# A hybrid decoder layer on one core: where the normalized rows are scaled, stored and cut

## The chip, the cores and the metric

The kernel runs on one core of one Trainium2 chip. A core has a matrix engine (PE, or TensorE), a vector engine (DVE), an activation engine (ACT), a general engine (POOL, or GpSimd), a queue engine that only starts transfers here (SP), and DMA engines that move data between device memory and the on-chip memory. Each engine works through its own queue in order; semaphores tie the queues together. The metric is the device time of one execution in microseconds (us); less is better.

## The reference

One decoder layer on 512 tokens of width 1024, all in float32. The input is normalized, and the normalized rows feed a token mixer with two branches and later serve as its residual:

```
h = layer_norm(x, ln_in_g, ln_in_b)
mix = token_mixer(h, ...)          # SSD branch and sliding-window attention branch, gated, projected
h = layer_norm(ALPHA * h + mix, ln_mix_g, ln_mix_b)
ffn = swiglu_ffn(h, ...)
h = layer_norm(ALPHA * h + ffn, ln_ffn_g, ln_ffn_b)
```

The attention has 16 heads of 64 columns over blocks of 128 queries, each block seeing its own block and the one before it, under a causal mask and a window mask.

## The kernel before

Tokens are cut in four tiles of 128 rows (`x_t[0]` to `x_t[3]`, 1024 columns each, in the tile `x_sb`). Weights stream in units of 128x1024: SP loads a unit into `w_raw`, ACT rounds it to `w_hi` (line 135), DVE forms the rest `w_lo` (line 136), and PE multiplies with three matmuls of 128x512 for each block of 128 (lines 149 to 151). PE's instruction order is the order of the program text. So is that of ACT and DVE in the first stage (lines 553 to 632). Elsewhere a scheduler orders the queues of ACT, DVE and POOL by priority and by when it expects an instruction to be ready, so an instruction far down in the text can come up early.

**First stage.** Four loads bring `x`. DVE takes mean and variance of tiles 0, 2 and 3 (`ln_stats`), ACT those of tile 1 (`act_stats`). Tiles 0 and 1 are normalized on ACT by `row_scale` (line 563), tiles 2 and 3 on DVE by `normalize` (line 201). `row_scale(1)` is called between the two halves of tile 3's statistics, so its ACT instruction stands ahead of the square root that tile 3 needs (line 197). Then `units.prepare(1)` splits the first weight unit `kv_w`, and `hT_tile(k)` transposes column block k of all four tiles on PE (line 217), rounds it on ACT (line 222) and forms the rest on DVE (lines 226 and 227). Dummy transposes (`warm_up`, line 548) fill PE before and between the first matmuls. Behind this stage POOL stores the four normalized tiles to device memory (`x_d`, line 635).

**Attention.** The loop over t has eight steps of two heads each. The scores are scaled on POOL (line 467), transposed on PE (line 480), copied to `pT` by ACT (line 482), masked by POOL (`affine_select`, line 483) and DVE (line 486), and multiplied with the values by PE (`ps_o`, line 493). Between these PE runs other products out of a list (`fill`, `need`): the q, x and gate products.

**Row scaling.** Behind the loop in the text POOL reads each stored tile back into `row` (line 703), multiplies it by the gain (line 704), adds the bias (line 705) and stores it to `h_d` (line 706), which is read again only for the residual of the mixer, far later. `row` has two buffers, which it shares with the scores `sc`; the gain and bias rows share buffers with `q_f`. After attention PE runs the products `yb` on `attT`, and then the SSD stage.

Of the kernel before, what the change touches and what calls it, by code (L numbers as in the profile page):

```python
# [14 lines left out]
AF = mybir.ActivationFunctionType  # L15
# [3 lines left out]
P = 128  # L19
S = 512  # L20
D = 1024
# [41 lines left out]
def kernel(  # L63
# [13 lines left out]
    nc = tc.nc  # L77
# [6 lines left out]
    def gap(pl, size):  # L84
# [13 lines left out]
        out=tri, in_=tri, pattern=[[1, P]], compare_op=ALU.is_ge, fill=0.0,  # L98
# [87 lines left out]
    def ln_stats(pl, src, between=None, cuts=(0, 512, 1024)):  # L186

        n = len(cuts) - 1
        st = pl.tile([P, 4, 6], F32, name="ln_st", tag="ln_st", bufs=2)[:, 0:n]
        for i in range(n):  # L190
            nc.vector.bn_stats(out=st[:, i], in_=src[:, cuts[i]:cuts[i + 1]])
            if i == 0 and between:
                between()
        mv = pl.tile([P, 2], F32, name="ln_mv", tag="ln_mv", bufs=3)
        nc.vector.bn_aggr(out=mv, in_=st)
        rs = pl.tile([P, 1], F32, name="ln_rs", tag="ln_rs", bufs=3)
        nc.scalar.activation(rs, mv[:, 1:2], AF.Sqrt, bias=eps_t, scale=1.0)
        return mv[:, 0:1], rs

    def normalize(src, mean, rs):  # L200
        nc.vector.tensor_scalar(
            out=src, in0=src, scalar1=mean, scalar2=rs, op0=ALU.subtract, op1=ALU.mult)
# [26 lines left out]
    def split_to(hi, lo, src):  # L229
        nc.scalar.copy(out=hi, in_=src)  # L230
        nc.vector.tensor_sub(out=lo, in0=src, in1=hi.bitcast(F32))

    x_d = dram.tile([S, D], F32, name="x_d")
# [35 lines left out]
    def axt(shape, name):  # L269
        return psX.tile(shape, F32, name=name, tag="ax")  # L270
# [111 lines left out]
    x_sb = at.tile([P, NT, D], F32, name="x_sb", tag="attT_lo")  # L382
# [86 lines left out]
        att_p[t] = sc  # L469
        yield  # L470

    att_p, last_exp = {}, [None]

    def weighted_values(t):
        kv, sc = t // 4, att_p.pop(t)
        pT = at.tile([P, 2, 7, P], F32, name="pT", tag="pT", bufs=1)
        for j in range(2):
            ps = axt([P, NT, P], "ps_pt")
            for n in range(NT):
                nc.tensor.transpose(ps[:, n], sc[:, j, n], ident)  # L480

            nc.scalar.copy(out=pT[:, j, 1::2], in_=ps[:, 1:])
            nc.gpsimd.affine_select(
                out=pT[:, j, 1::2], in_=pT[:, j, 1::2], pattern=[[0, NT - 1], [-1, P]], compare_op=ALU.is_ge,
                fill=0.0, base=-1, channel_multiplier=1)
            nc.vector.tensor_tensor(
                out=pT[:, j, 0::2], in0=ps, in1=tri.unsqueeze(1).broadcast_to([P, NT, P]), op=ALU.mult)
            yield
        ps = axt([P, S], "ps_o")
        for n in (0, 2, 1, 3):  # L490
            w = min(2, NT - n)
            for j in range(2):
                nc.tensor.matmul(  # L493
                    ps[64 * j:64 * j + 64, n * P:(n + w) * P], v_sb[:, n, kv * 64:kv * 64 + 64],
                    pT[:, j, 2 * n:2 * n + w].rearrange("p b k -> p (b k)"),
                    start=(n == 0), stop=(n == NT - 1))
        split_to(attT_hi[:, t], attT_lo[:, t], ps)
        yield
# [44 lines left out]
    x_t = [x_sb[:, ti] for ti in range(NT)]  # L543

    def warm_up(n):

        for _ in range(n):
            nc.tensor.transpose(ps_warm, ident, ident)

    def hT_tile(k, **kw):  # L550
        return transposed_k(psX, f_t[:, k % 3], x_t, k, 0, hT_hi[:, k], hT_lo[:, k], nc.vector, **kw)

    with tc.manual_schedule(engines={mybir.EngineType.DVE, mybir.EngineType.Activation}):

        nc.scalar.activation(at.tile([P, 1], F32, name="root"), eps_t, AF.Sqrt)
        warm_up(40)
        nmr = at.tile([P, NT + 1], F32, name="nmr")

        def row_scale(ti, mean, rs):
            nc.vector.reciprocal(rs, rs)  # L560
            nc.vector.scalar_tensor_tensor(
                out=nmr[:, ti:ti + 1], in0=mean, scalar=-1.0, in1=rs, op0=ALU.mult, op1=ALU.mult)
            nc.scalar.activation(x_t[ti], x_t[ti], AF.Identity, bias=nmr[:, ti:ti + 1], scale=rs)

        def act_stats(src):

            junk = f_t.rearrange("p a b -> p (a b)")[:, 0:D]
            mv = at.tile([P, 2], F32, name="ln_mv", tag="ln_mv", bufs=3)
            nc.scalar.activation(junk, src, AF.Identity, scale=1.0 / D, accum_out=mv[:, 0:1])
            nm = nmr[:, NT:NT + 1]  # L570
            nc.scalar.mul(out=nm, in_=mv[:, 0:1], mul=-1.0)
            nc.scalar.activation(junk, src, AF.Square, bias=nm, accum_out=mv[:, 1:2])
            rs = at.tile([P, 1], F32, name="ln_rs", tag="ln_rs", bufs=3)
            nc.scalar.activation(rs, mv[:, 1:2], AF.Sqrt, bias=eps_t, scale=1.0 / D)
            return mv[:, 0:1], rs

        row_scale(0, *ln_stats(at, x_t[0]))
        st1 = act_stats(x_t[1])
        st2 = ln_stats(at, x_t[2])
        st3 = ln_stats(at, x_t[3], partial(row_scale, 1, *st1))  # L580
        nc.vector.reciprocal(st2[1], st2[1])
        normalize(x_t[2], *st2)
        nc.vector.reciprocal(st3[1], st3[1])
        for a in (slice(0, 256), slice(256, D)):
            normalize(x_t[3][:, a], *st3)
        units.prepare(1)
        hT_tile(0, between=lambda i: warm_up(36 * (i == 0)))
        nc.scalar.copy(out=wdt_hi, in_=wdt_sb)
        nc.vector.tensor_sub(out=wdt_lo, in0=wdt_sb, in1=wdt_hi.bitcast(F32))
        units.prepare(2)  # L590
        hT_tile(1)
        units.prepare(3)
        w += [units.next(u, ahead=0) for u in (U_K, U_V, U_Q)]

        def part(k, o, a, b):

            nc.tensor.matmul(ps[o], w[o - 1][a][:, k], (hT_hi, hT_lo)[b][:, k],
                             start=k + a + b == 0, stop=k == KD - 1 and b == 1)

        def part_dt(k, b):  # L600

            nc.tensor.matmul(ps[0], wdt_r[:, k], (hT_hi, hT_lo)[b][:, k],
                             start=k + b == 0, stop=k == KD - 1 and b == 1)


        for o, a, b in ((1, 0, 0), (1, 1, 0), (2, 0, 0), (1, 0, 1), (2, 0, 1)):
            part(0, o, a, b)
            warm_up(3 * (b == 0))
        part_dt(0, 0)
        part_dt(0, 1)  # L610
        part(0, 2, 1, 0)
        for k in range(KD):
            if k > 0:

                for o in (1, 2):
                    for a in range(2):
                        part(k, o, a, 0)
                part_dt(k, 0)
                if k == 1:
                    part(0, 3, 0, 0)  # L620
                    part(0, 3, 0, 1)
                part(k, 3, 0, 0)
                part_dt(k, 1)
                for o in (1, 2):
                    part(k, o, 0, 1)
                if k == 1:
                    part(0, 3, 1, 0)
                part(k, 3, 1, 0)
                part(k, 3, 0, 1)
            if k + 2 < KD:  # L630
                dve_ins = hT_tile(k + 2)
            if k in (3, 5):
                units.prepare(4 + k // 5)
    for ti in range(NT):
        nc.gpsimd.dma_start(out=x_d[ti * P:(ti + 1) * P], in_=x_sb[:, ti])
    al_b = at.tile([P, NH], F32, name="al_b")
    snk = at.tile([P, 16], F32, name="snk")
    nsnk = at.tile([P, 16], F32, name="nsnk")
# [58 lines left out]
    gb1 = [at.tile([P, D], F32, name="gb1", tag="q_f", bufs=2) for _ in range(2)]  # L697
    for i, t in enumerate(gb1):
        nc.gpsimd.dma_start(out=t, in_=ln_in[i:i + 1].broadcast_to([P, D]))
    for ti in range(NT):  # L700
        row = at.tile([P, D], F32, name="row", tag="sc", bufs=2)
        rows = slice(ti * P, (ti + 1) * P)
        nc.gpsimd.dma_start(out=row, in_=x_d[rows])
        nc.gpsimd.tensor_mul(row, row, gb1[0])
        nc.gpsimd.tensor_add(row, row, gb1[1])
        nc.gpsimd.dma_start(out=h_d[rows], in_=row)

# [333 lines left out]
    for half in range(2):  # L1041
# [23 lines left out]
        for ti in toks:  # L1065
            hr = res[ti]
            for o in range(2):
                os = slice(o * 512, (o + 1) * 512)
                nc.vector.scalar_tensor_tensor(
                    out=hr[:, os], in0=hr[:, os], scalar=ALPHA, in1=acc[ti][o], op0=ALU.mult, op1=ALU.add)  # L1070
            mean, rs = ln_stats(r3, hr)
# [199 lines left out]
```

## Time and profile before

| what | value |
|---|---|
| median of 3 runs | 1038.83 us (1037.22 to 1038.92) |
| the profiled execution, its own time | 1038.49 us |
| its span, first to last instruction | 1036.6 us |
| mean granted TensorE clock | 0.995 |
| PE busy | 1017.7 us, 98% |
| DVE busy | 596.7 us, 58% |
| ACT busy | 506.1 us, 49% |
| POOL busy | 202.6 us, 20% |

The span is what the profile covers; the execution's own time is 1.9 us more. The busy times say which engine could be the bound; what a stage is worth is read from the waits inside that stage. A granted clock of 1.00 is TensorE at 2.4 GHz, 0.50 at 1.2 GHz.

### The profile page before, as it was taken

How to read it: one execution, taken by the hardware profiler on the slowest of the kernel's cores; microseconds unless marked ns; L12 is line 12 of the kernel's file. 1: busy time of each engine (PE TensorE's matmuls, PEld its weight loads, DVE VectorE, ACT ScalarE, POOL GpSimd, SP SyncE). 2: the span in 40 equal slices, each digit the busy share in tenths (PEclk: the TensorE clock that was granted, in tenths of full speed). 3: DMA queues.
4: the chain of work that ended last, by engine and by line, in shares of the span. 5: the costliest groups of instructions: out<-in, count | busy, mean ns of one | idle time of the engine just before them, and what ended most of it. 6: DMA issues, size and time to landing. Idle time of an engine off the chain costs nothing.

```text
span 1036.6 us, 13203 instructions
## 1 busy us (share of the span) xinstructions
PE 1017.7 (98%) x5044; PEld 839.0 (81%) x5044; DVE 596.7 (58%) x835; ACT 506.1 (49%) x864; POOL 202.6 (20%) x195
## 2 busy tenths in 40 slices
PE   8999999799999999999999999999999999999997
PEld 7888888588887878888888888898888888888885
DVE  6789875143666674685673676646433333332765
ACT  5464567624865785684652633334433332322450
POOL 2011224602215123102313730291000000000000
PEclk9999999899999999999999999999999999999999
DMA  8211224435343432334322254316433333331471
GB/s 314 82 62 62 87 83 135 149 123 158 103 131 96 144 127 98 104 116 139 119 93 82 82 183 162 122 41 208 157 121 105 120 107 117 121 122 61 153 252 43
DMA packets 38799, 126.56 MB, mean 122 GB/s; under 512 B 4528, under 2 KB 5040, under 8 KB 38480
## 3 DMA queue, kind: packets, MB, share of 16 engines
q1 hardware_dynamic: 36080, 116.14, 34.3%
q0 software_dynamic: 2080, 7.47, 2.1%
q10 hardware_dynamic: 576, 2.10, 0.5%
q8 instruction: 40, 0.66, 0.3%
q14 instruction: 23, 0.19, 0.1%
HBM read 119.27 MB, written 6.42 MB: 121 GB/s over the span
## 4 chain that ended last, share of the span: by engine, by line
PE 87%; DMA 3%; DVE 3%; ACT 2%; issue 1%; POOL 1%; SPq 0%; POOLq 0%; ACTq 0%; DVEq 0%
PE ps_mm L149 14%; PE ps_mm L150 13%; PE ps_mm L151 13%; PE ps_ff L149 8%; PE ps_ff L150 8%; PE ps_ff L151 8%; PE ps_da L149 2%; PE ps_da L151 2%; PE ps_da L150 2%; PE ps_mix L149 1%; PE ps_mix L151 1%; PE ps_mix L150 1%; PE ps_yd L836 1%; PE ps_o L493 1%; PE ps_db L150 1%
## 5 line engine op out<-in xcount | busy, mean ns | idle before, releaser
L135 ACT CAST w_hi<-w_raw 128x1024 fp32r<-128x1024 f32 x185 | 193.5, 1050 | 307.5 <-PE ps_ff L150 122.3
L136 DVE TENSOR_TENSOR w_lo<-w_raw,w_hi 128x1024 fp32r<-128x1024 f32 x185 | 234.7, 1273 | 159.0 <-ACT w_hi L135 155.0
L149 PE MATMUL ps_mm<-hT_hi,w_hi 128*128 128x512 f32 x504 | 203.8, 404 | 0.5 <-DVE cacc L371 0.5
L150 PE MATMUL ps_mm<-hT_lo,w_hi 128*128 128x512 f32 x504 | 197.1, 391 | 0.0
L151 PE MATMUL ps_mm<-hT_hi,w_lo 128*128 128x512 f32 x504 | 196.8, 390 | 0.0
L149 PE MATMUL ps_ff<-h2T_hi,w_hi 128*128 128x512 f32 (+1 forms) x384 | 143.2, 373 | 0.0
L150 PE MATMUL ps_ff<-h2T_lo,w_hi 128*128 128x512 f32 (+1 forms) x384 | 142.6, 371 | 0.0
L151 PE MATMUL ps_ff<-h2T_hi,w_lo 128*128 128x512 f32 (+1 forms) x384 | 142.6, 371 | 0.0
L149 PEld LDWEIGHTS ps_mm<-hT_hi,w_hi 128*128 128x128 f32 x504 | 95.0, 188 | 22.8 <-issue 5.1
L151 PEld LDWEIGHTS ps_mm<-hT_hi,w_lo 128*128 128x128 f32 x504 | 94.8, 188 | 20.4
L150 PEld LDWEIGHTS ps_mm<-hT_lo,w_hi 128*128 128x128 f32 x504 | 95.1, 189 | 18.2 <-issue 1.0
L151 PEld LDWEIGHTS ps_ff<-h2T_hi,w_lo 128*128 128x128 f32 x384 | 72.3, 188 | 12.6
L149 PEld LDWEIGHTS ps_ff<-h2T_hi,w_hi 128*128 128x128 f32 x384 | 72.3, 188 | 12.5
L150 PEld LDWEIGHTS ps_ff<-h2T_lo,w_hi 128*128 128x128 f32 x384 | 72.3, 188 | 12.4
L1119 DVE TENSOR_TENSOR sgf<-sgf,ps_ff 128x512 f32<-128x512 f32 x22 | 15.1, 687 | 68.0 <-PE ps_ff L151 68.0
L149 PE MATMUL ps_mm<-yh,w_hi 128*128 128x512 f32 x124 | 49.2, 397 | 0.0
L150 PE MATMUL ps_mm<-yl,w_hi 128*128 128x512 f32 x124 | 48.3, 390 | 0.0
L151 PE MATMUL ps_mm<-yh,w_lo 128*128 128x512 f32 x124 | 48.3, 389 | 0.0
L371 DVE SCALAR_TENSOR_TENSOR cacc<-ps_mm,pc,cacc 128x511 f32<-128x511 f32 (+2 forms) x54 | 39.9, 741 | 9.9 <-ACT cacc L368 9.3
L761 ACT ACTIVATE L<-L,nac 128x128 f32<-128x128 f32 x128 | 40.8, 390 | 5.9 <-POOL L L756 5.6
L780 DVE TENSOR_TENSOR L<-L,cb 128x1024 f32<-128x1024 f32 x16 | 21.7, 1354 | 37.2 <-ACT cb L778 22.0
L756 POOL TENSOR_SCALAR_AFFINE_SELECT L<-L 128x1024 f32<-128x1024 f32 x16 | 18.8, 1176 | 94.0 <-DMA L<-a_d 91.4
(269 smaller groups left out, 1724.3 us busy)
## 6 DMA issues: line engine op xcount, KB each, us to landing
w_raw<-in_wall_dram SPq DMA_DIRECT2D x187, 512.0 KB, 3.5
L<-a_d SPq DMA_DIRECT2D x16, 512.0 KB, 5.4
E<-e_d SPq DMA_DIRECT2D x24, 128.0 KB, 3.5
x_d<-x_sb POOLq DMA_DIRECT2D x4, 512.0 KB, 7.6
row<-x_d POOLq DMA_DIRECT2D x4, 512.0 KB, 4.1
h_d<-row POOLq DMA_DIRECT2D x4, 512.0 KB, 3.3
h_r<-h_d ACTq DMA_DIRECT2D x4, 512.0 KB, 4.2
out_dram<-y_o SPq DMA_DIRECT2D x7, 256.0 KB, 4.0
```

What stands on the lines that cost most here:

```text
L135: (copy or nc.scalar.copy)(out=hi, in_=w)
L136: self.last = (eng or nc.vector).tensor_sub(out=lo, in0=w, in1=hi.bitcast(F32))
L149: nc.tensor.matmul(ps, lh, rh, start=start, stop=False)
L150: nc.tensor.matmul(ps, lh, rl, start=False, stop=False)
L151: nc.tensor.matmul(ps, ll, rh, start=False, stop=stop)
L371: nc.vector.scalar_tensor_tensor(out=acc[:, d:], in0=ps[:, :S - d], scalar=pc[:, cw + 3 - d:cw + 4 - d], in1=acc[:, d:], op0=ALU.mult, op1 ...
L493: nc.tensor.matmul(ps[64 * j:64 * j + 64, n * P:(n + w) * P], v_sb[:, n, kv * 64:kv * 64 + 64], pT[:, j, 2 * n:2 * n + w].rearrange("p b k ...
L756: nc.gpsimd.affine_select(out=Lf, in_=Lf, pattern=[[0, 8], [1, P]], compare_op=ALU.is_ge, fill=-BIG, base=0, channel_multiplier=-1)
L761: nc.scalar.activation(L[:, j, t], L[:, j, t], AF.Exp, bias=nac5[:, g, j, c, t:t + 1], scale=1.0)
L780: nc.vector.tensor_tensor(out=Lf, in0=Lf, in1=cb.unsqueeze(1).broadcast_to([P, 8, P]), op=ALU.mult)
L836: nc.tensor.matmul(psd[64 * j:64 * j + 64, t], X[:, t, j], L[:, j, t], start=True, stop=True)
L1119: nc.vector.tensor_mul(sg, sg, pu)
```

## The change

1. The multiplication of each row tile by the gain is put behind the last `affine_select` of the attention loop on POOL's queue. It stays on POOL, as do the addition and the transfers.
2. The first store of a normalized tile to `x_d` waits for the DVE instruction that ends the last `hT_tile`.
3. Each normalization is cut in two pieces, columns 0 to 255 and 256 to 1023. On ACT the pieces of tiles 0 and 1 follow each other. On DVE the first pieces of tiles 2 and 3 come before the second pieces of both.

```
-    att_p, last_exp = {}, [None]
+    att_p, last_exp, last_sel = {}, [None], [None]
...
-            nc.gpsimd.affine_select(
+            last_sel[0] = nc.gpsimd.affine_select(
...
-            nc.scalar.activation(x_t[ti], x_t[ti], AF.Identity, bias=nmr[:, ti:ti + 1], scale=rs)
+            for a in pieces:
+                nc.scalar.activation(
+                    x_t[ti][:, a], x_t[ti][:, a], AF.Identity, bias=nmr[:, ti:ti + 1], scale=rs)
...
+        pieces = slice(0, 256), slice(256, D)
         row_scale(0, *ln_stats(at, x_t[0]))
         st1 = act_stats(x_t[1])
         st2 = ln_stats(at, x_t[2])
         st3 = ln_stats(at, x_t[3], partial(row_scale, 1, *st1))
         nc.vector.reciprocal(st2[1], st2[1])
-        normalize(x_t[2], *st2)
+        normalize(x_t[2][:, pieces[0]], *st2)
         nc.vector.reciprocal(st3[1], st3[1])
-        for a in (slice(0, 256), slice(256, D)):
-            normalize(x_t[3][:, a], *st3)
+        normalize(x_t[3][:, pieces[0]], *st3)
+        for ti, st in ((2, st2), (3, st3)):
+            normalize(x_t[ti][:, pieces[1]], *st)
         units.prepare(1)
...
+    late = mybir.DependencyInfo(mybir.DependencyClass.Sync, mybir.DependencyReason.DATA)
     for ti in range(NT):
-        nc.gpsimd.dma_start(out=x_d[ti * P:(ti + 1) * P], in_=x_sb[:, ti])
+        store = nc.gpsimd.dma_start(out=x_d[ti * P:(ti + 1) * P], in_=x_sb[:, ti])
+        if ti == 0:
+            tc.add_manual_dep(store.ins, dve_ins.ins.name, late, reason="loads")
...
         nc.gpsimd.dma_start(out=row, in_=x_d[rows])
-        nc.gpsimd.tensor_mul(row, row, gb1[0])
+        with tc.issue_after(last_sel[0].ins):
+            nc.gpsimd.tensor_mul(row, row, gb1[0])
         nc.gpsimd.tensor_add(row, row, gb1[1])
```

## Rows read from the trace of the kernel before

**Rows 1.** Who waited for whom, PE only: total us, times, longest
```profile
PE ps_o L493 <- POOL pT L483: 6.6, 1, 6.6
```

**Rows 2.** Timeline of PE, 184 to 204 us: start, duration, instruction, idle before
```profile
191.36 3.72 PE L493 MATMUL ps_o<-pT,v_sb 128*64 128x256 f32 x16 [6.58 <-POOL pT L483]
195.01 0.80 PE L149 MATMUL ps_mm<-hT_hi,w_hi 128*128 128x512 f32 x1
...
196.85 0.40 PE L150 MATMUL ps_mm<-hT_lo,w_hi 128*128 128x512 f32 x1
...
203.45 0.39 PE L149 MATMUL ps_mm<-attT_hi,w_hi 128*128 128x512 f32 x1
```

**Rows 3.** Timeline of PE, 168 to 174 us, the same step one t earlier
```profile
170.33 1.74 PE L493 MATMUL ps_o<-pT,v_sb 128*64 128x256 f32 x16
172.00 0.50 PE L149 MATMUL ps_mm<-hT_hi,w_hi 128*128 128x512 f32 x1
...
173.03 0.40 PE L150 MATMUL ps_mm<-hT_lo,w_hi 128*128 128x512 f32 x1
```

**Rows 4.** Windows: stretch, busy us and instructions by engine, granted clock, DMA
```profile
191.36:195.01 3.65, 3.65 (x17) 2.17 (x17) 0.00 (x0) 0.00 (x0) 2.02 (x3) 0.50 0.74 287
```

**Rows 5.** Timeline of POOL, 159 to 213 us
```profile
169.09 2.38 POOL L704 TENSOR_TENSOR row<-row,gb 128x1024 f32<-128x1024 f32 x1 [2.52 <-DMA row<-x_d]
...
180.71 0.54 POOL L703 DMA_DIRECT2D row<-x_d  x1 [2.68 <-DMA h_d<-row]
185.46 2.34 POOL L704 TENSOR_TENSOR row<-row,gb 128x1024 f32<-128x1024 f32 x1 [4.21 <-DMA row<-x_d]
...
190.77 1.00 POOL L483 TENSOR_SCALAR_AFFINE_SELECT pT<-pT 128x384 f32<-128x384 f32 x2
```

**Rows 6.** Timeline of ACT, 160 to 215 us
```profile
179.76 0.84 ACT L482 COPY pT<-ps_pt 128x384 f32<-128x384 f32 x2
```

**Rows 7.** Timeline of DVE, 9 to 19 us
```profile
12.54 0.81 DVE L201 TENSOR_SCALAR x_sb<-x_sb,ln_mv,ln_rs 128x1024 f32<-128x1024 f32 x1
13.27 0.15 DVE L583 RECIPROCAL ln_rs<-ln_rs 128x1 f32<-128x1 f32 x1
13.46 1.00 DVE L201 TENSOR_SCALAR x_sb<-x_sb,ln_mv,ln_rs 128x256 f32<-128x256 f32 x2
14.38 1.22 DVE L136 TENSOR_TENSOR kv_w<-w_raw,kv_w 128x1024 fp32r<-128x1024 f32 x1
```

**Rows 8.** Chain of work that ended last, 0 to 20 us: start, duration, what
```profile
13.79 0.43 DVE x_sb L201
```

**Rows 9.** Timeline of ACT, 6 to 17.5 us
```profile
11.67 1.24 ACT L563 ACTIVATE x_sb<-x_sb,nmr,ln_rs 128x1024 f32<-128x1024 f32 x1 [0.46 <-DVE nmr L561]
12.81 0.28 ACT L197 ACTIVATE ln_rs<-ln_mv,eps_t 128x1 f32<-128x1 f32 x1
13.11 1.05 ACT L135 CAST kv_w<-w_raw 128x1024 fp32r<-128x1024 f32 x1
```

**Rows 10.** Timeline of PE, 15 to 19 us
```profile
18.57 0.50 PE L597 MATMUL ps_v<-hT_hi,kv_w 128*128 128x512 f32 x1 [0.27 <-DVE kv_w L136]
```

**Rows 11.** Timeline of DVE, 0 to 75 and 160 to 215 us
```profile
36.83 0.69 DVE L227 TENSOR_TENSOR hT_lo<-f_t,hT_hi 128x512 fp32r<-128x512 f32 x1
...
74.33 0.69 DVE L231 TENSOR_TENSOR attT_lo<-ps_o,attT_hi 128x512 fp32r<-128x512 f32 x1 [0.51 <-ACT attT_hi L230]
...
184.01 1.23 DVE L136 TENSOR_TENSOR w_lo<-w_raw,w_hi 128x1024 fp32r<-128x1024 f32 x1 [2.46 <-ACT w_hi L135]
```

**Rows 12.** Timeline of POOL, 0 to 75 and 75 to 330 us
```profile
60.79 2.04 POOL L467 TENSOR_TENSOR sc<-sc,sm 128x512 f32<-128x512 f32 x2 [45.50 <-DVE sm L465]
...
248.42 2.73 POOL L797 TENSOR_TENSOR Xd<-X,dec 128x256 f32<-128x256 f32 x3 [39.38 <-DVE X L786]
```

**Rows 13.** DMA issues: queue, count, KB each, median us to landing
```profile
x_d<-x_sb POOLq DMA_DIRECT2D x4, 512.0 KB, 7.6
```

**Rows 14.** Line 464, DVE: ns min/median/max, first and last start
```profile
L464 DVE TENSOR_TENSOR sm<-sm,es x8: 157/168/2310, 60.2 to 169.2; 128x8 f32<-128x8 f32 x8
```

## The prediction made before the run

> **What bounds the kernel now.** I read the list of waits for PE first, since PE is the engine that nearly fills the span. It holds one wait of size: the value products `ps_o` wait 6.6 us, once, for POOL's masks on `pT` [rows 1]. PE's timeline gives the place: PE could have started at 191.36 - 6.58 = 184.78 and starts at 191.36 [rows 2]. This is the last step, t = 7, of the attention loop.
>
> POOL's timeline says why. The two masks run at 190.77. Their input was there much earlier, as ACT ended its two copies to `pT` at 179.76 + 0.84 = 180.60 [rows 6]. In between POOL's queue holds row scaling: a reload of `row` at 180.71 that first waited 2.68 us for a store, a multiplication at 185.46 that waited 4.21 us for that reload, then the addition and another reload [rows 5]. POOL takes its queue in order, so the masks waited for transfers that they don't need.
>
> Nothing hides this wait, since PE's order is that of the text. It also has a tail. During `ps_o` the granted clock is 0.50 [rows 4], the 1.2 GHz level, after PE had been idle for 6.58 us. So the same 16 matmuls take 195.01 - 191.36 = 3.65 us, against 172.00 - 170.33 = 1.67 us one step earlier [rows 2, 3]. The next four matmuls, start to start, take 196.85 - 195.01 = 1.84 us against 173.03 - 172.00 = 1.03 us [rows 2, 3].
>
> The second place to read is the start. The chain of waits runs there through DVE: it normalizes from 12.54, splits `kv_w` at 14.38 [rows 7, 8], and the split of the second `kv_w` unit is what PE waits for at 18.57, with 0.27 us of idle [rows 10]. PE's wait list names nothing larger behind that until `ps_o`, so a delay of DVE here delays everything behind it one for one.
>
> **Part 1, the scaling behind the last mask.** No instruction is added or removed; four multiplications, and with them the additions and stores that need them, move behind the masks. What may stay ahead is the reload of the first two tiles into the two buffers of `row`, some 0.54 us of POOL each [rows 5], with their inputs long stored. A third reload needs a store, which needs a multiplication, so it can't stand ahead of the masks any more. The masks can then run at 180.60 and take 1.00 us [rows 5]: done at 181.6, some 3.2 us before PE asks at 184.78. Two reload issues in front, 1.1 us, still fit. The gain is the whole wait and its tail: 6.58 + (3.65 - 1.67) + (1.84 - 1.03) = 6.58 + 1.98 + 0.81 = 9.37 us.
>
> What is late next? The scaled rows themselves. Even if all four tiles went one after the other, each with reload (0.54 + 4.21), two operations of 2.34 to 2.38, a store issue of about 0.54 and a wait of 2.68 for it [rows 5], that is about 12.7 us a tile and 51 us in all: the end would come near 233. POOL's next work, `Xd`, stood at 248.42 after 39.38 us of idle [rows 12], and would come about 9 us earlier, near 240. The rows are free by then, and `h_d` is read only by the mixer's residual, far later. So the move costs nothing on the path; without that idle time it would cost what it overruns.
>
> Beside the scaling, DVE works on weights. Line 464 shows what that can mean: 2310 ns where its median is 168 ns [rows 14]; it began at 169.19, just behind the multiplication of 169.09 to 171.47 [rows 5]. So one small DVE operation was held for one POOL operation. I take nothing for this in the sum, since `w_lo` is made two units before its use: the one at 184.01 [rows 11] serves the product that starts at 203.45 [rows 2]. The bounds are nothing and the slow rival below.
>
> The Trainium skill, page "SBUF — State Buffer", section "Who interferes with whom", speaks against putting POOL work beside DVE: a DVE instruction with two inputs in SBUF and a POOL instruction that reads SBUF share a read port, and whichever comes second is blocked for the whole of the other. The row of line 464 agrees, with 2.31 us for one such meeting; by the rule as by the row the sum stays the same unless such meetings follow one another without a break.
>
> **Part 2, the stores held back.** The first `x_d` store moves behind the DVE instruction that ends at 36.83 + 0.69 = 37.5 [rows 11]. Behind it on POOL wait the three other stores, or they go ahead; either way POOL's next instruction stood at 60.79 after 45.50 us of idle [rows 12]. With four issues of about 0.54 us and 7.6 us to landing [rows 13] the last lands near 48. Its buffer is taken over by `attT_lo`, first written at 74.33 [rows 11], and the first reloaded tile was multiplied at 169.09 [rows 5]. The cover is 26 us; without it POOL's masks or that write would be late by the overrun. What could it gain? The early stores shared the DMA engines with the first loads, but the DVE and ACT rows from 11.67 on show no wait for a transfer [rows 7, 9], so I take 0. The bounds are a gain of 0.5 us, if the loads ahead of 9.3 us were slowed after all, and a loss of one landing, 7.6 us, if a weight load were held; I stay at zero, since weights are loaded four units ahead.
>
> **Part 3, the pieces.** On ACT tile 0's second piece falls into idle time. Tile 1's doesn't: the square root for tile 3 stands behind both pieces. Now it starts at 12.81, after one instruction at 11.67 [rows 9]. An extra ACT instruction costs its fixed part. The nearest row is the one-column square root, 0.28 us, 0.30 us to the next start; the large one hands over 0.10 us before its end (1.24 against 12.81 - 11.67 = 1.14) [rows 9]. That gives 0.18 to 0.30 us; I take 0.25, nearer the upper end because this form has two per-row operands where the root has one. The root then ends at 13.06 + 0.28 = 13.34.
>
> On DVE the first piece of tile 2 takes 13.79 - 13.46 = 0.33 us [rows 7, 8], so it ends at 12.54 + 0.33 = 12.87, and DVE now idles until the root is there. Before, the whole of tile 2 filled that time (0.73 us, to 13.27 [rows 7]). Then, start to start: reciprocal at 13.37, 0.19 to the first piece of tile 3 (13.46 - 13.27), 0.33 for it, 0.59 (14.38 - 13.79) for each of the two large pieces: 13.37 + 0.19 + 0.33 + 0.59 + 0.59 = 15.07 for the split of `kv_w`, which stood at 14.38. That is 0.69 us later. With ACT's cost at its ends it is 0.62 to 0.74; were ACT free of charge, the reciprocal could come at 13.12 and the loss would still be 0.44.
>
> The first transposes gain nothing either: column block 0 needs tile 3's first piece, now at 13.56 instead of 13.46. As DVE's chain then runs without a break to 18.57, PE loses 0.69 us.
>
> **Sum.** -9.37 + 0.69 = -8.68 us. The profiled execution took 1038.49 us, so 1029.8 us. The median of the runs is 0.34 us above that execution, well inside their spread of 1.7 us. A measurement of this kernel can tell a change from none at about 0.2%, or 2.1 us.
>
> **Rivals.**
> - *The pieces cost nothing* (or the early loads gain a little): DVE's order matters less than I read, for instance if PE's dummy transposes absorb it. Then 1038.49 - 9.37 = 1029.1 us. For it speaks that PE's idle time at 18.57 is only 0.27; against it, that DVE's rows from 12.54 to 14.38 stand end to end [rows 7] and lead to that wait.
> - *The clock falls at the start.* PE's idle time before 18.57 grows from 0.27 to about 0.96 us, and with it the risk of the 1.2 GHz level. One such fall cost 1.98 + 0.81 = 2.79 us at `ps_o`: 1029.8 + 2.8 = 1032.6 us. Against it: the only fall shown followed 6.58 us of idle.
> - *The change doesn't do what it says*: the masks stay late because something else in POOL's queue holds them, say a reload that waits. Then only the pieces remain: 1038.49 + 0.69 = 1039.2 us, the same. Against it: no reload ahead of the masks has anything left to wait for.
> - *Slower: DVE is shut out while POOL scales.* The place is `w_lo` of the first `yb` product, ready to start at 184.0. If the eight operations ran from 182.3 almost without a gap, with 5 issues among them, they would end at 182.3 + 8 x 2.38 + 5 x 0.57 = 204.2. Were DVE held to the very end, `w_lo` would end at 205.4, while PE would ask at 203.45 - 9.37 + 0.69 = 194.8: a wait of 10.6 us and another 2.79 for the clock, less 8.68, is 4.7 us more than before: 1043.2 us. It decides the sign once `w_lo` ends later than 194.8 + 5.9 = 200.7. Against it: line 464 was held by one operation, not by a row of them, and the reloads of tiles 3 and 4 leave POOL idle for microseconds.
>
> **How the numbers follow.** Forecast 66%, pieces free 14%, clock at the start 9%, no effect 6%, DVE shut out 5%. Time 1029.8 us. The range reaches over the first three cases, 1029.1 to 1032.6, 89% together, and some of the spread of the runs on either side: 1027.8 to 1033.2 us. Faster by over 0.2%: 0.66 + 0.14 + 0.09 = 0.89; within 0.2%: 0.06; slower: 0.05.
>
> **What would show it.** Right: the wait of `ps_o` for the masks is gone from PE's list; `ps_o` at t = 7 takes about 1.7 us at a granted clock of 1.00; all four multiplications stand behind the last mask, and the last `h_d` store lands before 233; the split of `kv_w` starts near 15.1 and `ps_v` near 19.3, behind a longer idle on DVE ahead of tile 3's reciprocal; four stores stand near 38 on POOL with nobody waiting. Wrong: a new wait of PE for `w_lo` or for a weight load between 185 and 240, `Xd` waiting for `row`, or a granted clock under 1.00 before 25.

## The result, and the profile after

The changed kernel takes 1030.13 us (median of 4 runs, 1029.61 to 1030.6) against 1038.38 us for the kernel before beside it: ratio 0.9922, 95% interval 0.9905 to 0.9939, so 8.2 us less. The forecast was 1029.8 us. The profiled execution took 1030.6 us, with a span of 1028.6 us and a mean granted clock of 0.996.

The list of waits for PE in the changed kernel (total us, times, longest):

```profile
PE ps_warm L548 <- POOL ident masks.py:199: 1.5, 1, 1.5
PE ps_tr L217 <- DVE x_sb L201: 1.0, 2, 0.7
PE ps_db L150 <- DVE w_lo L136: 0.6, 1, 0.6
PE ps_mm L149 <- DVE cacc L371: 0.5, 1, 0.5
```

The 6.6 us of `ps_o` [rows 1] are gone. What stands high in the list now lies at the start (`ps_tr`, waiting for pieces of `x`) and near the end (`ps_db`, at 1005.9 us, which was 1013.9 in the kernel before). The timeline of PE at the place of the old wait, in the changed kernel:

```profile
185.81 1.73 PE L493 MATMUL ps_o<-pT,v_sb 128*64 128x256 f32 x16
187.47 0.50 PE L149 MATMUL ps_mm<-hT_hi,w_hi 128*128 128x512 f32 x1
...
188.51 0.40 PE L150 MATMUL ps_mm<-hT_lo,w_hi 128*128 128x512 f32 x1
...
195.09 0.39 PE L149 MATMUL ps_mm<-attT_hi,w_hi 128*128 128x512 f32 x1
```

And the window over `ps_o` (busy us of PE, PEld, DVE, ACT, POOL, then granted clock, DMA share, GB/s):

```profile
185.81:187.47 1.66, 1.66 (x17) 1.06 (x16) 1.66 (x1) 1.64 (x3) 1.66 (x2) 1.00 0.00 0
```

No idle time stands in front of `ps_o`, it runs at a granted clock of 1.00 where it had 0.50 [rows 4], and the next four matmuls take 188.51 - 187.47 = 1.04 us. Against [rows 2], `ps_o` starts 5.55 us earlier, the matmul behind it 7.54 us, the one at 188.51 8.34 us. The shift then stays near -8.34 us up to that place. POOL's timeline of the changed kernel shows where the rows went:

```profile
180.94 0.60 POOL L712 DMA_DIRECT2D row<-x_d  x1 [7.08 <-issue]
181.56 1.00 POOL L483 TENSOR_SCALAR_AFFINE_SELECT pT<-pT 128x384 f32<-128x384 f32 x2
182.52 2.40 POOL L714 TENSOR_TENSOR row<-row,gb 128x1024 f32<-128x1024 f32 x1
185.00 2.37 POOL L715 TENSOR_TENSOR row<-row,gb 128x1024 f32<-128x1024 f32 x1
187.34 3.39 POOL L714 TENSOR_TENSOR row<-row,gb 128x1024 f32<-128x1024 f32 x1
...
212.47 0.58 POOL L716 DMA_DIRECT2D h_d<-row  x1 [0.30 <-POOL row L715]
240.05 2.73 POOL L807 TENSOR_TENSOR Xd<-X,dec 128x256 f32<-128x256 f32 x3 [27.00 <-DVE X L796]
```

The second reload stands right ahead of the masks and costs 0.60 us. The masks run at 181.56, 9.2 us earlier than in [rows 5]. All four multiplications follow them, the last store is issued at 212.47, and POOL is idle for 27 us before `Xd`. So the stall became idle time of POOL that nobody waits for.

DVE at the start, in the changed kernel:

```profile
8.94 1.29 DVE L191 BATCH_NORM_STATS2 ln_st<-x_sb 128x6 f32<-128x512 f32 x2 [2.61 <-DMA x_sb<-in_x_dram]
...
11.20 0.69 DVE L191 BATCH_NORM_STATS2 ln_st<-x_sb 128x6 f32<-128x512 f32 x1
...
12.19 0.41 DVE L201 TENSOR_SCALAR x_sb<-x_sb,ln_mv,ln_rs 128x256 f32<-128x256 f32 x1
13.05 0.16 DVE L587 RECIPROCAL ln_rs<-ln_rs 128x1 f32<-128x1 f32 x1 [0.45 <-ACT ln_rs L197]
13.25 1.59 DVE L201 TENSOR_SCALAR x_sb<-x_sb,ln_mv,ln_rs 128x256 f32<-128x256 f32 x3
14.76 1.22 DVE L136 TENSOR_TENSOR kv_w<-w_raw,kv_w 128x1024 fp32r<-128x1024 f32 x1
```

and ACT there, with the two pieces of tile 1 in one row:

```profile
11.32 1.52 ACT L564 ACTIVATE x_sb<-x_sb,nmr,ln_rs 128x256 f32<-128x256 f32 x2 [0.37 <-DVE nmr L561]
12.74 0.28 ACT L197 ACTIVATE ln_rs<-ln_mv,eps_t 128x1 f32<-128x1 f32 x1
```

The pair of pieces holds the square root for 12.74 - 11.32 = 1.42 us, where one instruction took 1.14 [rows 9]: a piece more costs ACT 0.28 us. DVE finishes tile 2's small piece and then idles 0.45 us for that root. Yet `kv_w` is split only 14.76 - 14.38 = 0.38 us later than before [rows 7], since the first row of this fence, tile 2's statistics, stands at 8.94, not where the kernel before has it:

```profile
9.29 1.29 DVE L191 BATCH_NORM_STATS2 ln_st<-x_sb 128x6 f32<-128x512 f32 x2 [3.03 <-DMA x_sb<-in_x_dram]
```

Both rows wait for tile 2's load, so the load landed earlier in this execution.

PE's windows at the start, columns as in the window above:

```profile
16.00:18.00 2.00, 1.97 (x8) 1.63 (x9) 1.97 (x4) 1.72 (x3) 0.00 (x0) 0.56 1.05 375
18.00:20.00 2.00, 2.00 (x7) 1.60 (x6) 1.97 (x3) 0.00 (x0) 0.00 (x0) 0.59 0.93 279
```

Here the granted clock is 0.56 and 0.59, where the kernel before had 1.00. The window of the kernel before, then the transposes of column block 2 in it and in the changed kernel:

```profile
16.00:18.00 2.00, 2.00 (x12) 1.42 (x10) 1.97 (x4) 1.97 (x3) 0.00 (x0) 1.00 1.05 414
18.91 0.60 PE L217 MATMUL ps_tr<-ident,x_sb 128*128 128x128 f32 x4
20.01 0.60 PE L217 MATMUL ps_tr<-ident,x_sb 128*128 128x128 f32 x4
```

They start 1.10 us later. The low clock is the one thing in the trace that the forecast had called a sign of being wrong. The stores, on POOL's timeline of the changed kernel:

```profile
13.15 0.74 POOL L642 DMA_DIRECT2D x_d<-x_sb  x1 [8.33 <-ACT ln_rs L197]
14.57 1.10 POOL L642 DMA_DIRECT2D x_d<-x_sb  x2 [0.68 <-DMA snk<-in_sinks_dram]
38.91 0.53 POOL L642 DMA_DIRECT2D x_d<-x_sb  x1 [23.24 <-DVE hT_lo L227]
```

Only the store that was told to wait does so. The other three went ahead of it.

The difference of the two traces, along PE: +1.10 us at the start, -8.34 - 1.10 = -9.44 us at the stall and its tail, +0.36 near the end: -7.98 us.

### The profile page after: what moved, and what is told of

The parts are those of the page before. It is cut to its first block, busy times and chain, and to the rows that moved or that the text cites. A ratio compares the mean times of both kernels' runs of the same rounds, so it can differ in the third digit from the quotient of the medians.

```text
span 1028.6 us, 13207 instructions
## 1 busy us (share of the span) xinstructions
PE 1016.1 (99%) x5044; PEld 838.8 (82%) x5044; DVE 601.9 (59%) x836; ACT 506.5 (49%) x866; POOL 206.2 (20%) x195
## 4 chain that ended last, share of the span: by engine, by line
PE 90%; DMA 3%; ACT 2%; DVE 2%; POOL 1%; issue 1%; SPq 0%; ACTq 0%; POOLq 0%; DVEq 0%
PE ps_mm L149 14%; PE ps_mm L150 14%; PE ps_mm L151 14%; PE ps_ff L151 8%; PE ps_ff L150 8%; PE ps_ff L149 8%; PE ps_da L151 2%; PE ps_da L150 2%; PE ps_da L149 2%; PE ps_mix L149 1%; PE ps_mix L151 1%; PE ps_mix L150 1%; PE ps_db L150 1%; PE ps_db L151 1%; PE ps_o L493 1%; PE ps_db L149 1%
## 5 line engine op out<-in xcount | busy, mean ns | idle before, releaser
L136 DVE TENSOR_TENSOR w_lo<-w_raw,w_hi 128x1024 fp32r<-128x1024 f32 x185 | 241.4, 1310 | 155.9 <-ACT w_hi L135 153.7
L1129 DVE TENSOR_TENSOR sgf<-sgf,ps_ff 128x512 f32<-128x512 f32 x22 | 15.1, 685 | 68.0 <-PE ps_ff L151 68.0
```

The lines of the kernel that those rows point to most:

```text
L136: self.last = (eng or nc.vector).tensor_sub(out=lo, in0=w, in1=hi.bitcast(F32))
L1129: nc.vector.tensor_mul(sg, sg, pu)
```

## The experiments

The theory to be tested was the sum of the forecast: the scaling saves 9.4 us by itself, the stores do nothing, the pieces cost 0.7 us through the root that ACT hands to DVE. Its rivals were that the low clock at the start belongs to the pieces, and that POOL's operations shut DVE out.

### One part at a time

**e1_scaling**: the kernel before, with the scaling moved.

```
+            last_sel[0] = nc.gpsimd.affine_select(
...
+        with tc.issue_after(last_sel[0].ins):
+            nc.gpsimd.tensor_mul(row, row, gb1[0])
```

> The kernel before with part 1 alone: the multiplications stand behind the last mask, nothing else is changed. My theory, that the wait of ps_o and its slow tail are the whole gain: 9.4 us less, about 1029.0 us, ps_o of t = 7 free of a wait at a granted clock of 1.00, and the first stage as before (ps_tr of column block 2 at 18.9 us, granted clock 1.00 throughout). Rival, that the later stores or the pieces carry part of the gain: 1030.5 us or more.

Measured: 1028.96 us, ratio 0.9915 (0.9902 to 0.9929). PE's timeline of this kernel:

```profile
184.62 1.74 PE L493 MATMUL ps_o<-pT,v_sb 128*64 128x256 f32 x16
186.29 0.50 PE L149 MATMUL ps_mm<-hT_hi,w_hi 128*128 128x512 f32 x1
```

In its trace PE runs 0.06 us earlier than before ahead of `ps_o` and 9.53 us earlier behind it: the move saves 9.47 us, and it is the whole gain. Side by side the medians are 8.3 us apart; the interval, 7.4 to 10.2 us, holds both.

**e2_stores**: the kernel before, with the first store held.

```
+        if ti == 0:
+            tc.add_manual_dep(store.ins, dve_ins.ins.name, late, reason="loads")
```

> The kernel before with part 2 alone: one store held until the last hT_tile. In the changed kernel x tile 2 was there at 8.92 us where it was 9.27 before. My theory, that the early store of tile 0 ran beside the last x loads and slowed them: x tile 2 at about 8.9 us again, the whole first stage 0.35 us earlier, 1038.0 us, the same by the clock. Rival, that the landing only varies from one execution to the next: about 9.3 us and no change in the first stage.

Measured: 1038.43 us, ratio 1.0007 (0.9998 to 1.0015): no difference that shows in the time. In the trace one store is held (37.49), three go ahead (12.88 twice, 14.43), as in the changed kernel. The statistics of tile 2 begin at 8.78 instead of 9.29, and `kv_w` is split at 14.04 instead of 14.38; whether the store did that is taken up below the table. That 0.34 us is not in the measured time; PE's shift shrinks to -0.15 us by the end, at two short waits near 370 and 1013 us whose lengths differ from execution to execution in every kernel here.

**e3_pieces**: the kernel before, with the pieces alone, on ACT and on DVE.

```
-        normalize(x_t[2], *st2)
+        normalize(x_t[2][:, pieces[0]], *st2)
...
+        for ti, st in ((2, st2), (3, st3)):
+            normalize(x_t[ti][:, pieces[1]], *st)
```

> The kernel before with part 3 alone: each normalization in pieces of 256 and 768 columns. My theory: DVE reaches the first split of kv_w 0.7 us later (15.1 instead of 14.4 us), PE stands idle for more of the time from 14 to 16 us, its granted clock falls to 0.5 to 0.6 between 16 and 20 us, and ps_tr of column block 2 comes 1.1 to 1.5 us later (20.0 to 20.4 instead of 18.9): 1039.5 to 1039.9 us. Rival, that the low clock in the changed kernel was an accident of that execution: the clock stays 1.00, ps_tr at 19.6, 1039.1 us.

Measured: 1038.49 us, ratio 1.0012 (1.0003 to 1.0020): 0.3 to 2.1 us slower. The part that expected a low clock missed: between 14 and 20 us this execution shows 1.00.

**e4_no_pieces**: the changed kernel, with the normalization uncut again (the edit of e3_pieces undone).

> The changed kernel without the pieces (parts 1 and 2). My theory, by which the three parts add up: -9.4 for the scaling, -0.35 for the store, nothing lost at the start: 1028.7 us, about 1.4 us under the changed kernel, ps_tr of column block 2 at 18.6 us at a granted clock of 1.00. Rival, that the pieces cost nothing that lasts: 1030.1 us, as the changed kernel.

Measured: 1028.8 us, ratio 0.9915 (0.9901 to 0.9929). It is ahead of the changed kernel by 1.3 us of medians; but the two were not measured beside each other, and the kernel before beside them took 1037.3 us here and 1038.38 us there. By the ratios it is ahead by 0.7 us. It is level with e1_scaling.

### The start

**e5_start_filled**: the changed kernel, with dummy transposes in PE's gaps at the start.

```
-        hT_tile(0, between=lambda i: warm_up(36 * (i == 0)))
+        hT_tile(0, between=lambda i: warm_up((36, 2, 6, 0)[i]))
...
-        hT_tile(1)
+        hT_tile(1, between=lambda i: warm_up(3 * (i == 3)))
...
-            warm_up(3 * (b == 0))
+            warm_up((5 if a == 0 and o == 1 else 3) * (b == 0))
```

> The changed kernel with 13 more dummy transposes on PE in the idle times of the first stage: 2 and 6 between the transposes of column block 0, 3 behind those of block 1, 2 more behind the first matmul. My theory, that the low clock of the changed kernel's start follows PE's idle time: granted clock 1.00 from 12 to 22 us and ps_tr of column block 2 at about 19.3 us (20.0 in the changed kernel); 0.7 us less than it, about 1029.4 us. Rival, that the dummies only delay PE: ps_tr at 20.0 or later.

Measured: 1029.83 us, ratio 0.9927 (0.9911 to 0.9944), granted clock 1.00 from 14 to 20 us. By itself this decides nothing, because e7_double and e8_after_again (below) have the same first stage without the filling and show 1.00 as well.

**e9_root_first**: the changed kernel, with tile 1's large piece on ACT put behind the root for tile 3.

```
-        st3 = ln_stats(at, x_t[3], partial(row_scale, 1, *st1))
+        st3 = ln_stats(at, x_t[3], partial(row_scale, 1, *st1, 1))
+        nc.scalar.activation(
+            x_t[1][:, pieces[1]], x_t[1][:, pieces[1]], AF.Identity, bias=nmr[:, 1:2], scale=st1[1])
```

> The changed kernel with tile 1's second piece moved behind the square root that tile 3 needs. My theory, that DVE's loss at the start is 0.5 us of waiting for that root and 0.2 us for one more instruction: the reciprocal of tile 3 follows the first piece of tile 2 without idle time, the split of kv_w starts 5.6 us behind the first statistics of tile 2 instead of 5.8 (before: 5.1), so 0.2 to 0.5 us earlier than in the changed kernel. Rival, that the root isn't what DVE waits for: no change on DVE.

Measured: 1029.5 us, ratio 0.9924 (0.9909 to 0.9939), not to be told from the changed kernel. Its DVE timeline:

```profile
10.92 0.69 DVE L191 BATCH_NORM_STATS2 ln_st<-x_sb 128x6 f32<-128x512 f32 x1
...
11.91 0.41 DVE L201 TENSOR_SCALAR x_sb<-x_sb,ln_mv,ln_rs 128x256 f32<-128x256 f32 x1
12.24 0.15 DVE L589 RECIPROCAL ln_rs<-ln_rs 128x1 f32<-128x1 f32 x1
12.43 1.59 DVE L201 TENSOR_SCALAR x_sb<-x_sb,ln_mv,ln_rs 128x256 f32<-128x256 f32 x3
14.06 1.23 DVE L136 TENSOR_TENSOR kv_w<-w_raw,kv_w 128x1024 fp32r<-128x1024 f32 x1
```

The idle time in front of the reciprocal is gone: with the root ready early, DVE goes from piece to piece. So the root is what DVE waits for in the changed kernel.

**e8_after_again** and **e10_no_pieces_again**: the changed kernel and e4_no_pieces once more, side by side on one chip.

> The changed kernel a second time, beside the same kernel without the pieces on one chip. Theory (the pieces cost DVE 0.73 us between tile 2's statistics and the split of the first weight unit, and nothing gives it back): 0.7 us slower than the kernel without pieces, some 1029.7 against 1029.0 us; tile 2's statistics to the split 5.82 us. Theory that the low granted clock at the start comes from the pieces: a clock near 0.56 between 16 and 20 us again, and 1.4 us slower than the kernel without pieces. Theory that it was an accident of one execution: a clock of 1.00 there most likely.

> The changed kernel without the pieces (parts 1 and 2 alone) a second time. Theory: tile 2's statistics to the split of the first weight unit 5.1 us, and a time 0.7 us under that of the changed kernel on the same chip. Rival (the pieces cost nothing in the end): the same time within 0.2 us.

Measured: 1029.88 us, ratio 0.9925 (0.9911 to 0.9938), and 1028.7 us, ratio 0.9914 (0.9900 to 0.9927). The intervals overlap, but over both pairs the nine runs with the pieces lie from 1028.4 to 1031.0 and the eight without from 1028.3 to 1029.6, with medians 1.2 to 1.3 us apart (1.2 in this pair). That is more than the 0.7 us of the theory, but not by more than such runs differ. The window of e8_after_again that answers to the low one above:

```profile
16.00:18.00 2.00, 1.94 (x11) 1.46 (x11) 1.97 (x4) 1.50 (x2) 0.00 (x0) 1.00 1.04 352
```

The same kernel, and this time the granted clock is 1.00.

The twelve profiled executions together (starts in us; tile 2's statistics, the second half of tile 3's statistics, the split of `kv_w`, the transposes of column block 2; clock of the window from 16 to 18 us):

| execution | first store | pieces | tile 2 | tile 3 | split | split - tile 3 | block 2 - split | clock |
|---|---|---|---|---|---|---|---|---|
| before | early | no | 9.29 | 11.55 | 14.38 | 2.83 | 4.53 | 1.00 |
| e1_scaling | early | no | 9.23 | 11.49 | 14.32 | 2.83 | 4.53 | 1.00 |
| e6_wait_filled | early | no | 9.20 | 11.46 | 14.29 | 2.83 | 5.30 | 0.50 |
| e3_pieces | early | yes | 9.03 | 11.29 | 14.86 | 3.57 | 4.53 | 1.00 |
| e2_stores | held | no | 8.78 | 11.21 | 14.04 | 2.83 | 4.54 | 1.00 |
| e4_no_pieces | held | no | 8.66 | 10.95 | 13.78 | 2.83 | 4.54 | 1.00 |
| e10_no_pieces_again | held | no | 8.16 | 10.64 | 13.48 | 2.84 | 4.53 | 1.00 |
| after | held | yes | 8.94 | 11.20 | 14.76 | 3.56 | 5.25 | 0.56 |
| e5_start_filled | held | yes | 8.90 | 11.17 | 14.73 | 3.56 | 4.53 | 1.00 |
| e7_double | held | yes | 8.82 | 11.08 | 14.64 | 3.56 | 4.53 | 1.00 |
| e8_after_again | held | yes | 8.55 | 10.98 | 14.54 | 3.56 | 4.53 | 1.00 |
| e9_root_first | held | yes, root first | 8.60 | 10.92 | 14.06 | 3.14 | 5.22 | 0.50 |

Three things separate here. The pieces cost DVE 3.56 - 2.83 = 0.73 us in every execution, of which e9_root_first gets back 0.42. In the eight executions with a held first store the second half of tile 3's statistics begins at 11.02 us in the mean, in the four without at 11.45, so 0.43 us later; the two groups don't overlap, though by only 0.08 us. And the low clock costs 0.7 to 0.8 us where it comes, which is in three executions out of twelve: one with the changed kernel's first stage, one with the root first, and one (e6_wait_filled) with the first stage of the kernel before.

That the early store made the loads of `x` later is not shown; the traces speak against it. First the DMA queues that moved anything in the first 12 us of the kernel before, and its store; then ACT's first work on tile 1 in e3_pieces, and the store there:

```profile
q1 hardware_dynamic: 1256, 3.26, 78.8%
7.85 0.74 POOL L635 DMA_DIRECT2D x_d<-x_sb  x1 [3.03 <-ACT x_sb L563]
7.77 1.06 ACT L571 ACTIVATE f_t<-x_sb 128x1024 f32<-128x1024 f32 x1
7.97 0.74 POOL L639 DMA_DIRECT2D x_d<-x_sb  x1 [3.17 <-DMA x_sb<-in_x_dram]
```

POOL's queue (q0) is not among them: in the four executions with the early store its first packet starts between 12.25 and 12.50 us, and the last tile of `x` has landed by 10.51 us. The difference is older than the store, too. By the traces' semaphores tile 1 lands at 7.75 to 8.02 us in these four, about when the store is issued (7.85 to 8.02), and in e3_pieces before it; in the eight others it lands at 6.79 to 7.67. From the landing of tile 1 to that of tile 2 it takes 1.24 to 1.34 us in all twelve. What brings tile 1 earlier in the eight is open.

### The tail of the wait

**e6_wait_filled**: the kernel before, with 56 dummy transposes in the time in which PE waits for the masks. The wait stays; of PE's idleness all but 0.87 us goes.

```
+        if t == NQ - 1:
+            ps_fill = axt([P, P], "ps_fill")
+            for _ in range(56):
+                nc.tensor.transpose(ps_fill, ident, ident)
         ps = axt([P, S], "ps_o")
```

> The kernel before with 56 dummy transposes on PE (6.4 us of them) right ahead of the ps_o that waits; the masks stay late. My theory, that 2.8 us of the gain are a lower clock behind the idle time: ps_o still starts near 191.4 us, but its 16 matmuls take 1.7 us at a granted clock of 1.00 instead of 3.65 at 0.50, and the kernel takes 2.8 us less than before. Rival, that ps_o was slow for another reason, such as its operands' buffers or the transfers running then: 3.65 us again and no gain.

Measured: 1035.88 us, ratio 0.9987 (0.9977 to 0.9996): 1.3 us less. PE's timeline of this kernel:

```profile
185.31 6.27 PE L492 MATMUL ps_fill<-ident 128*128 128x128 f32 x56
192.46 2.19 PE L497 MATMUL ps_o<-pT,v_sb 128*64 128x256 f32 x16 [0.87 <-POOL pT L483]
194.59 0.50 PE L149 MATMUL ps_mm<-hT_hi,w_hi 128*128 128x512 f32 x1
```

and its windows there:

```profile
184.00:191.00 7.00, 7.00 (x60) 6.71 (x59) 1.22 (x1) 6.06 (x8) 4.43 (x2) 1.00 0.38 134
191.00:193.00 2.00, 1.13 (x10) 0.61 (x10) 0.00 (x0) 0.00 (x0) 1.99 (x5) 1.00 0.24 43
193.00:197.00 4.00, 4.00 (x26) 2.97 (x26) 0.69 (x1) 0.85 (x2) 2.30 (x2) 1.00 0.61 241
```

With PE busy the granted clock stays at 1.00 through `ps_o`, and PE's shift against the kernel before goes from +1.10 us at the start of `ps_o` to -1.25 us behind the slow stretch (197 to 300 us): 2.35 us, of the 2.79 us that the forecast had put down to the clock. The four matmuls behind `ps_o` give back all of their 0.81 us (195.62 - 194.59 = 1.03). `ps_o` itself still takes 194.59 - 192.46 = 2.13 us at a granted clock of 1.00, against 1.67 us where nothing was waited for; so 0.46 us of its slowness has another cause, which is open. The +1.10 us ahead of it are the other reason why the profiled execution is only 1.4 us shorter: 0.7 us of it is the low clock at its start, the rest masks that came 0.42 us later. The measured gain is short of the 2.8 us expected (interval 0.4 to 2.4 us).

### POOL beside DVE

**e7_double**: the changed kernel, with every multiplication and every addition of the rows made twice.

```
             nc.gpsimd.tensor_mul(row, row, gb1[0])
+            nc.gpsimd.tensor_mul(row, row, gb1[0])
+        nc.gpsimd.tensor_add(row, row, gb1[1])
         nc.gpsimd.tensor_add(row, row, gb1[1])
```

> The changed kernel with every multiplication and every addition of the row scaling done twice (the residual rows change by that): 8 more POOL operations of 2.4 us behind the masks. My theory, that the scaling has room there: no more time than the changed kernel, 1029.5 to 1030.6 us, w_lo held by 2.1 us at each meeting and PE without a new wait, the last h_d store near 232, Xd still at 240. Rival, that DVE is shut out for long: PE waits for w_lo between 185 and 240 and the time rises by 3 us or more.

Measured: 1029.96 us, ratio 0.9928 (0.9914 to 0.9943), as the changed kernel. First the weight splits of DVE in the changed kernel itself, where POOL has eight operations:

```profile
179.04 1.23 DVE L136 TENSOR_TENSOR w_lo<-w_raw,w_hi 128x1024 fp32r<-128x1024 f32 x1 [4.23 <-ACT w_hi L135]
185.10 3.36 DVE L136 TENSOR_TENSOR w_lo<-w_raw,w_hi 128x1024 fp32r<-128x1024 f32 x1 [2.46 <-ACT w_hi L135]
191.42 3.37 DVE L136 TENSOR_TENSOR w_lo<-w_raw,w_hi 128x1024 fp32r<-128x1024 f32 x1 [1.28 <-ACT w_hi L135]
```

and then POOL and the longest split in e7_double, where POOL has sixteen:

```profile
184.13 2.38 POOL L715 TENSOR_TENSOR row<-row,gb 128x1024 f32<-128x1024 f32 x1
186.46 3.41 POOL L714 TENSOR_TENSOR row<-row,gb 128x1024 f32<-128x1024 f32 x1
...
211.60 3.38 DVE L136 TENSOR_TENSOR w_lo<-w_raw,w_hi 128x1024 fp32r<-128x1024 f32 x1 [0.17 <-ACT w_hi L135]
...
235.26 0.58 POOL L718 DMA_DIRECT2D h_d<-row  x1 [0.30 <-POOL row L717]
239.18 2.73 POOL L809 TENSOR_TENSOR Xd<-X,dec 128x256 f32<-128x256 f32 x3 [3.35 <-DVE X L798]
```

Even with twice the work on POOL no split took over 3.38 us, and PE's list has no wait for `w_lo` between 185 and 240 us. Here DVE is held for one POOL operation at a time, never for a row of them. POOL's idle time before `Xd` fell from 27.0 to 3.35 us: the doubled work just fits.

## Why the prediction was right

**The scaling: right, in mechanism and size.** -9.37 us was forecast; the changed kernel shows -9.44 and e1_scaling alone -9.47. The split of it holds too: e1_scaling takes wait and tail away together, and e6_wait_filled takes most of the tail away alone: 2.35 us, against 1.98 + 0.81 = 2.79 us. So the clock is shown for five sixths of the tail; the rest, some 0.45 us in `ps_o` itself, goes only with the wait, for a reason that no run shows. One reload ahead of the masks, 0.60 us, was within the 3.2 us of margin that the forecast gave it.

**The pieces: right, slightly low.** +0.69 us was forecast through a chain of ACT's extra piece (0.25 us; measured 0.28), DVE idle for the root (0.5; measured 0.45) and the later split; measured 0.73 us, inside the 0.62 to 0.74 given. e9_root_first confirms the middle of the chain. The split stands at 14.76 and not near 15.1 because the tiles of `x` landed earlier in this execution.

**The stores: 0 stands in the time, but not as described.** I took 0, with a gain of 0.5 us as the bound, and e2_stores allows a gain of at most 0.2 us. The reason that I weighed, stores that share the DMA engines with the first loads, is not what the traces show: only the store of tile 0 was early, and its first packet started at 12.25 us, when all of `x` had landed. The 0.43 us between the two groups of executions is there before the store is issued, so I can't put it down to the store. What came later where the store was early is a weight load: the second unit, beside which the store's packets ran, landed at 15.2 to 15.4 us in those four executions and at 12.7 to 13.3 in the eight others. PE's start didn't pay for that: from the split to the transposes of block 2 it is 4.53 to 4.54 us in both groups wherever the clock is 1.00. The four stores didn't stand together near 38 either. One did; POOL's order let the other three pass at 13 to 15 us.

**The rivals.** *The pieces cost nothing* falls with the table, which shows the 0.73 us in every execution; in the time itself the loss stays at the edge of what these runs can tell (0.3 to 2.1 us in e3_pieces, overlapping intervals in e8_after_again and e10_no_pieces_again). *No effect* falls with the list of waits. *DVE shut out* had its premise confirmed (four splits between 185 and 210 us took 2.63 to 3.37 us instead of 1.22) and its conclusion refuted, since the splits are made two units ahead and each is held once. The Trainium skill, page "SBUF — State Buffer", section "Who interferes with whom", has the second of the two blocked for the whole of the other; the split of 185.10 agrees, as it ends 1.09 us after the POOL operation that ends at 187.37. *The clock falls at the start* came true in the profiled execution, but neither for the reason nor at the price given. The reason was to be PE's longer idle time, which comes with the pieces; yet four of the six executions with pieces have a clock of 1.00 from 16 to 18 us (one of them, e5_start_filled, with PE's gaps filled), and one without them has 0.50. Nor does PE's idle time just ahead sort them: from 14 to 16 us PE is busy for 1.31 us in the changed kernel and 1.28 us in e8_after_again, which keeps 1.00, and for 1.57 us both in e6_wait_filled, whose clock falls, and in the kernel before, whose clock doesn't. The price was 0.7 us, not 2.8; with it `ps_v` came at 19.78 instead of the 19.3 of the forecast. What sets it off is not settled, nor why it costs less here; that part of it falls in time in which PE would have waited for DVE is only argued.

**The sum.** That the changes in the profiled execution come so near to the forecast of -8.68 us is partly luck, as smaller terms cancel: -9.44 (scaling) - 0.35 (tile 3's statistics at 11.20 instead of 11.55) + 0.73 (pieces) + 0.72 (low clock, 5.25 - 4.53) + 0.36 (waits near the end) = -7.98 us. Tile 3's statistics and the last two are not shown to come from the change. e8_after_again, without the low clock, has +0.16 us at the start and -9.47 us at the stall, and from there to the end gives back 0.69 us on balance, mostly at short waits near 370 and 1013 us; it ends at -8.62 us.

By the medians the fastest version here is the change without its pieces, or the scaling alone: 1028.7 to 1029.0 us. The intervals overlap with that of the whole change.

## What to carry to other kernels

When an engine waits for a small operation whose input has long been ready, read what stands ahead of it in that engine's queue: here work that nobody needed soon kept PE idle, and the slow stretch behind 6.58 us of idle time added another 2.79 us, of which 2.35 went when PE was kept busy. Before cutting an operation into pieces, look who is next in the queue of the engine that gets the extra instruction; here it was a 0.28 us root on which another engine's whole chain hung. Where a profile shows something new at a place that a change touched, look at the same place in other executions, of the kernel before too, before putting it down to the change; and look whether the supposed cause stands ahead of its effect. Both the low clock and the earlier loads would have passed for effects of the change in one pair of traces.

## What the runs showed of the hardware that was not expected

- The granted clock at the start (16 to 18 us) was 0.50 to 0.56 in three of twelve executions and 1.00 in nine, with the same first stage giving either.
- POOL and DVE hold each other by turns. The split at 185.10 ended with 188.46 after a POOL operation that ended at 187.37, and the next POOL operation, started at 187.34, took 3.39 us instead of 2.40, about 1 us more.
- The 512 KB store that POOL issued at 7.85 us moved its first packet at 12.25 us, behind all loads of `x` (the last landed at 10.51). In the four executions with an early store it took 4.4 to 4.5 us.
- `ps_o` took 2.13 us at a granted clock of 1.00 behind a wait of 0.87 us (e6_wait_filled), against 1.67 us without a wait.
